# A decoder layer's weight stream: eight raw buffers of half a unit in place of four of a whole unit

## The chip, the cores and the metric

The kernel runs on one core of one Trainium2 chip. The metric is the device time of one execution in microseconds (us), the median of several runs. The core has a matrix engine (TensorE, PE in the profile; PEld is its weight load), a vector engine (VectorE, DVE), an activation engine (ScalarE, ACT), GpSimd (POOL) and SyncE (SP), which here issues nearly all loads. Transfers run on 16 DMA engines.

## The reference

A decoder layer on 256 tokens of width 1024, all in f32: a SwiGLU feed-forward, a token mixer, a second feed-forward, each behind an RMS normalisation whose shift, scale and gate come from a conditioning vector c.

```
mod = silu(c) @ w_ada + b_ada                      # 9 vectors of 1024: sh1 sc1 gt1 ... sh3 sc3 gt3
n = rmsnorm(h, g1) * (1 + sc1) + sh1
h = h + 0.5 * gt1 * ((silu(n @ w1_gate) * (n @ w1_up)) @ w1_down)        # d_ff = 2816
n = rmsnorm(h, g_mix) * (1 + sc2) + sh2
u, q, k, v = split(n @ w_in)
h = h + gt2 * (concat(pool(u), dilated_attention(q, k, v)) @ w_out)      # 8 heads of 64
n = rmsnorm(h, g2) * (1 + sc3) + sh3
h = h + 0.5 * gt3 * ((silu(n @ w2_gate) * (n @ w2_up)) @ w2_down)
out = rmsnorm(h, g_final)
```

Every matrix is f32. The kernel keeps that precision on PE by writing a matrix as a rounded part and the rest, w = hi + lo, and by three products for each: x_hi w_hi + x_lo w_hi + x_hi w_lo.

## The kernel before, in words

**Units.** The host packs all weights into 114 units of 1 MB, w[i] with 128 rows of 2048 f32 (8 KB a row), in the order in which they are used. `plan()` writes this order. Kinds of units: `ada` (two 128-column pieces of w_ada, transposed), `lead` (one eighth of the depth of four gate/up column chunks), `gu` (half the depth of one gate/up chunk), `down`, `win`, `wout`. In the first feed-forward, units 0 to 7 are ada, lead 0, ada, lead 1, ada, lead 2, ada, lead 3; two gu units follow, then ada and lead in turn again up to lead 7.

**Load and cast.** `fetch()` takes the next unit: it takes a tile `raw` of [128, 2048] from a pool of RAW = 4 buffers and SP issues one load into it (L250). For an ada unit, DVE multiplies each half with the row vector cb = silu(c) and sums along the row (L255), which gives one column of `mod` a half. For any other unit each half of 1024 columns is cast on ACT into a tile `hi` (L266), and DVE subtracts, lo = raw - hi (L267); `hi` and `lo` have PARTS = 11 buffers of half a unit each. A raw buffer goes back to the pool when both of its halves have been read, and the next load in the order waits for it on SP. `want()` fetches up to AHEAD = 5 units beyond the one that is asked for.

**The start.** Units 0 and 1 are loaded by hand, each with two loads of half a unit (L507), and a block under `in_order()` fixes the order of the first instructions of each engine as written. Unit 1's casts stand there (L544 to L555). `casts_after` keeps later casts behind that block.

**Lead steps.** For j = 0 to 3 and then 4 to 7, `lead_mod` turns two columns of mod into scale and shift (acol, L344), writes the normalised and modulated activations of depth slice j (nha on ACT, L424, then n32l on ACT and nla on DVE), and `lead_step` runs 24 matmuls (L445) on them with the lead unit: 4 chunks, 2 row tiles of 128 tokens, 3 products.

**The rest.** `ffn_chunk` (L370 to L372) and `down` (L411) run the remaining feed-forward, chunk by chunk. `finish1` and `finish2` close a sub-layer for one row tile of 128 tokens: the residual on DVE (L364, L366), squares on ACT (L294), the root on POOL (L296 to L300), scaled rows xs on ACT (L319), which PE transposes (L307). Their instructions are issued under `urgent()`, a high priority.

**Order.** Each engine executes its own queue in order. The order in a queue is fixed at compile time by a planner, which goes by the order of the code, by priorities, by added dependencies (`order_dep`, `casts_after`) and by its own model of how long loads and instructions take; it also gives out the pool buffers.

Of the kernel before, what the change touches and what calls it, by code (L numbers as in the profile page):

```python
# [10 lines left out]
F32 = mybir.dt.float32  # L11
# [4 lines left out]
P = 128  # L16
S = 256
NT = S // P
D = 1024
# [21 lines left out]
WF1 = (1, 22)  # L41
WMIX = (0, 8)
WLEAD = (0, 4)
RAW = 4
SPIN = (4, 8, 8, 5)
PARTS = 11
PAD = 336
# [8 lines left out]
def plan():  # L56
    def pairs(m):
        return [("ada", (m * KD + 2 * i, m * KD + 2 * i + 1)) for i in range(KD // 2)]

    def both(sc, sh):  # L60
        return [("ada", (sc * KD + j, sh * KD + j)) for j in range(KD)]

    def ffn(f, first):
        units = []
        for ci in range(first, NCH):
            units += [("gu", (f, ci, 0)), ("gu", (f, ci, 1))]
            if 0 < ci < NCH - HOLD + 1:
                units.append(("down", (f, ci - 1)))
        return units + [("down", (f, ci)) for ci in range(NCH - HOLD, NCH)]

    def weave(main, extra, start, stop):

        out, done = [], 0
        for i, u in enumerate(main):
            out.append(u)
            upto = min(max(i + 1 - start, 0), stop - start) * len(extra) // (stop - start)
            out += extra[done:upto]
            done = max(done, upto)
        return out

    order = []
    first, third = both(SC1, SH1), both(SC3, SH3)
    for j in range(KD):
        if j == KD // 2:
            order += [("gu", (0, ci, 0)) for ci in (4, 5)]
        order += [first[j], ("lead", (0, j))]
    f1 = [("gu", (0, ci, 1)) for ci in (2, 3)] + [("down", (0, ci)) for ci in FIRST[:-1]]
    f1 += [u if u != ("down", (0, 5)) else ("down", (0, FIRST[-1])) for u in ffn(0, 6)]
    order += weave(f1, pairs(GT1) + both(SC2, SH2) + pairs(GT2)[:EARLY], *WF1)
    mix = [("win", (ci, h)) for ci in (1, 2, 3, 0) for h in range(2)] + [("wout", i) for i in WOUT]  # L90
    order += weave(mix, pairs(GT2)[EARLY:] + third[:KD // 2], *WMIX)
    order += weave([("lead", (1, j)) for j in range(KD)], third[KD // 2:], *WLEAD)
    f2 = ffn(1, LEAD)
    f2 = f2[:2] + [("down", (1, ci)) for ci in range(LEAD - 1)] + f2[2:]
    order += weave(f2, pairs(GT3), 8, len(f2) - 8)
    return order
# [73 lines left out]
def block_kernel(ctx, tc, w, vec, x, c, gf, wpool, bandd, biasd, out):  # L170
    nc = tc.nc
    order = plan()
# [3 lines left out]
    lay = ctx.enter_context(tc.tile_pool(name="lay", bufs=1))  # L176
    rawp = ctx.enter_context(tc.tile_pool(name="rawp", bufs=RAW))
    hip = ctx.enter_context(tc.tile_pool(name="hip", bufs=PARTS))
# [38 lines left out]
    ready = {}  # L217
    bulk = []
    queues = {}
    done_mod = set()  # L220
    place = {u: i for i, u in enumerate(order)}

    def order_dep(late, early, reason):
        tc.add_manual_dep(late, early.name, mybir.DependencyInfo(
            mybir.DependencyClass.NoSync, mybir.DependencyReason.DATA), reason=reason)

    def behind(cast, unit, kind):

        units, first = queues.get(cast.ins.engine, ((1e9, 1e9), None))
        if unit >= units[kind]:  # L230
            order_dep(cast.ins, first, "casts later")

    def casts_after(firsts, units):

        for f in firsts:
            queues[f.engine] = (units, f)
        for cast in bulk:
            if any(cast[0].ins.engine == f.engine for f in firsts):
                behind(*cast)

    def note(cast, unit, kind):
        bulk.append((cast, unit, kind))
        behind(cast, unit, kind)

    def fetch():
        i = pos[0]
        pos[0] += 1
        kind, a = order[i]
        raw = rawp.tile([P, 2048], F32, name=f"raw{i}", tag="raw")
        nc.sync.dma_start(raw, w[i])  # L250
        if kind == "ada":
            with tc.high_priority(offset=ADA if i >= 2 * KD else 0):
                for s, m in enumerate(a):
                    r = raw[:, ts(s, D)]
                    note(nc.vector.tensor_tensor_reduce(  # L255
                        r, r, cb, 1.0, vecs[:, m:m + 1], ALU.mult, ALU.add, mod[:, m:m + 1]), i, 1)
                    done_mod.add(m)
            return
        his, los = [], []
        for s in range(2):  # L260
            hi = hip.tile([P, 1024], F32R, name=f"hi{i}_{s}", tag="hi")
            lo = lop.tile([P, 1024], F32R, name=f"lo{i}_{s}", tag="lo")
            n = 1024 // (2 if i in (1, 2 * KD - 1) else 1)
            for o in range(0, 1024, n):
                src = raw[:, s * 1024 + o:s * 1024 + o + n]
                note(nc.scalar.copy(hi[:, o:o + n], src), i + s / 2, 0)  # L266
                note(nc.vector.tensor_tensor(lo[:, o:o + n], src, hi[:, o:o + n].bitcast(F32), ALU.subtract), i + s / 2, 0)  # L267
            his.append(hi)
            los.append(lo)
        ready[(kind, a)] = (his, los)  # L270
# [206 lines left out]
                down(f, ci, 1, hid[ci][1], accs[1], banks)  # L477


    @contextmanager  # L480
    def in_order():

        traced = nc.cur_bb.bb.instructions
        done, last = len(traced), {}
        yield last
        for i in traced[done:]:
            if i.engine in last:
                order_dep(i, last[i.engine], "in order")
            last[i.engine] = i

    spin_ps = accp.tile([P, 2 * P], F32, name="spin", tag="acc")
    spin_in = ident.bitcast(mybir.dt.bfloat16)

# [7 lines left out]
    def x_keep(t, b, pt):  # L501
        nc.scalar.copy(xT[b][:, :, ts(t, P)], pt)

    raw = [rawp.tile([P, 2048], F32, name=f"raw{i}", tag="raw") for i in range(2)]
    for r, ww in zip(raw, (w[0], w[1])):
        for s in range(2):
            nc.sync.dma_start(r[:, ts(s, D)], ww[:, ts(s, D)])  # L507
    pos[0] = 2
    his = [hip.tile([P, 1024], F32R, name=f"hi1_{s}", tag="hi") for s in range(2)]
    los = [lop.tile([P, 1024], F32R, name=f"lo1_{s}", tag="lo") for s in range(2)]  # L510
# [4 lines left out]
    with in_order() as last:  # L515
        spin(SPIN[0])
        for b in range(2):
            pc = psp.tile([P, 512], F32, name=f"pc{b}", tag="ps")
            mm(pc, ones, crow[:, ts(b, 512)], start=True, stop=True)
            nc.scalar.activation(cb[:, ts(b, 512)], pc, AF.Silu)  # L520
        for t in range(NT):
            spin(SPIN[1 + t])
            xs.append(hip.tile([P, D], F32, name=f"xs{t}", tag="hi"))
            v = tiny.tile([P, 1], F32, name=f"vx{t}", tag="v")
            ht = h[:, ts(t, D)]
            nc.vector.tensor_tensor_reduce(xs[t], ht, ht, 1.0, D * EPS, ALU.mult, ALU.add, v)
            rs.append(tiny.tile([P, 1], F32, name=f"rx{t}", tag="r"))
            nc.gpsimd.tensor_tensor(rs[t], v, mhalf, ALU.pow)
            x_rows(t, 0)
            turned.append(turn(xs[t][:, 0:512], f"xt{t}0"))  # L530
        spin(SPIN[3])
        nc.vector.tensor_scalar(gains, vecs[:, G1:PS], float(D) ** 0.5, None, ALU.mult)
        for s, m in enumerate(order[0][1]):
            r = raw[0][:, ts(s, D)]
            nc.vector.tensor_tensor_reduce(r, r, cb, 1.0, vecs[:, m:m + 1], ALU.mult, ALU.add, mod[:, m:m + 1])
            done_mod.add(m)
        scale_cols(0, SC1, 0, 1)
        a, sh = acol[:, 0:1], mod[:, SH1 * KD:SH1 * KD + 1]
        n32 = work.tile([P, S], F32, name="n32l00", tag="t2", bufs=T2)
        for q in range(4):  # L540
            src = raw[1][:, ts(q, 512)]
            hi, lo = his[q // 2][:, ts(q % 2, 512)], los[q // 2][:, ts(q % 2, 512)]
            if q == 0:
                nc.vector.tensor_copy(hi, src)  # L544
                for t in range(NT):
                    nc.scalar.activation(n1[t][0][:, 0, :], turned[t][:, 0, :], AF.Identity, bias=sh, scale=a)
                    nc.vector.tensor_scalar(n32[:, ts(t, P)], turned[t][:, 0, :], a, sh, ALU.mult, ALU.add)
                for t in range(NT):
                    nc.vector.tensor_tensor(n1[t][1][:, 0, :], n32[:, ts(t, P)], n1[t][0][:, 0, :].bitcast(F32),
                                            ALU.subtract)  # L550
            else:
                nc.scalar.copy(hi, src)
                if q < 3:
                    x_keep(q - 1, 0, turned[q - 1])
            nc.vector.tensor_tensor(lo, src, hi.bitcast(F32), ALU.subtract)  # L555
    casts_after([last[e] for e in last if e in (nc.scalar.engine, nc.vector.engine)], (2, 2))


    nm = {}
# [305 lines left out]
```

## Time and profile before

| | before |
|---|---|
| median of 3 runs | 494.17 us (493.03 to 494.2) |
| profiled execution, its own time | 494.21 us |
| span of the profiled execution | 492.4 us |
| mean granted clock of TensorE | 0.993 |
| loads of units | 112 of 1024 KB, 4 of 512 KB |
| weight queue (q1) | 17568 packets, 121.25 MB, 65.0% of 16 engines |
| bytes read from HBM | 124.61 MB, 255 GB/s over the span with the bytes written |

The span runs from the first to the last instruction; the time of an execution lies some 1.8 us above it. Lines such as L266 are lines of the kernel before. A row of the timeline or of a group names the engine, the line, the operation, the tile that it writes and the tiles that it reads (out<-in), and in brackets the engine's idle time before it and what ended that. SPq and ACTq are the queues that issue loads.

### The profile page before, as it was taken

What the parts mean: (1) busy time and instruction counts of PE and PEld (TensorE: products, weight loads), DVE (VectorE), ACT (ScalarE), POOL (GpSimd) and SP (SyncE); (2) the same over time, 40 slices, a digit from 0 to 9 for tenths busy, and PEclk for the clock granted to TensorE, in tenths of its full rate; (3) what the DMA queues carried; (4) which work ended last, traced back from release to release, by engine and by line L of the source; (5) the groups of instructions that cost most, each with busy time, mean ns of one, the idle gap of its engine ahead of it and who ended that gap; (6) DMA issues with size and microseconds to landing.
All of it is one profiled execution on the core that took longest, in us unless ns stands there. A gap on an engine that the chain in (4) does not pass through costs nothing.

```text
span 492.4 us, 5990 instructions
## 1 busy us (share of the span) xinstructions
PE 479.4 (97%) x2176; PEld 385.1 (78%) x2176; DVE 354.8 (72%) x569; ACT 260.0 (53%) x437; POOL 15.6 (3%) x26
## 2 busy tenths in 40 slices
PE   8999999999999999899999999999999999999994
PEld 5778888888888887778767888888878888888883
DVE  5978989996897896787868776755666756655244
ACT  4776575553544354574677468945543443544121
POOL 1000000000000002120000012000000000000000
PEclk9999999999999999899999999999999999999998
DMA  8999995997987995859775848285367749540002
GB/s 306 400 359 315 369 338 203 369 425 281 396 325 286 338 385 193 309 198 405 317 244 184 298 154 318 106 321 197 126 236 253 281 189 341 180 162 9 35 2 85
DMA packets 20383, 126.05 MB, mean 256 GB/s; under 512 B 2409, under 2 KB 4225, under 8 KB 6018
## 3 DMA queue, kind: packets, MB, share of 16 engines
q1 hardware_dynamic: 17568, 121.25, 65.0%
q10 hardware_dynamic: 2786, 4.43, 2.6%
q8 instruction: 17, 0.28, 0.2%
q14 instruction: 12, 0.10, 0.1%
HBM read 124.61 MB, written 1.06 MB: 255 GB/s over the span
## 4 chain that ended last, share of the span: by engine, by line
PE 87%; DMA 5%; DVE 2%; ACT 2%; POOL 2%; issue 2%; POOLq 0%; DVEq 0%; ACTq 0%
PE accf L411 22%; PE gu L370 9%; PE le L445 9%; PE gu L371 9%; PE gu L372 9%; PE ld L445 6%; PE accm L762 5%; DMA raw<-in_w_dram 4%; PE zp L370 3%; PE zp L372 3%; PE zp L371 3%; PE ht L397 2%; DMA h<-in_x_dram 1%; ACT hi L266 1%; PE sh L370 1%
## 5 line engine op out<-in xcount | busy, mean ns | idle before, releaser
L267 DVE TENSOR_TENSOR lo<-raw,hi 128x1024 fp32r<-128x1024 f32 (+1 forms) x156 | 184.4, 1208 | 45.4 <-ACT hi L266 37.0
L266 ACT CAST hi<-raw 128x1024 fp32r<-128x1024 f32 (+1 forms) x156 | 158.3, 1041 | 78.9 <-PE accf L411 24.9
L255 DVE CUSTOM_DVE_ANT_0 raw<-raw,cb,vecs 128x1024 f32<-128x1024 f32 x70 | 88.1, 1279 | 4.8 <-DMA raw<-in_w_dram 4.8
L411 PE MATMUL accf<-hi,hh 128*128 128x512 f32 x176 | 56.3, 396 | 0.2
L411 PE MATMUL accf<-lo,hh 128*128 128x512 f32 x176 | 56.3, 394 | 0.0
L411 PE MATMUL accf<-hi,hl 128*128 128x512 f32 x176 | 55.7, 390 | 0.0
L370 PE MATMUL gu<-hi,nhc 128*128 128x512 f32 x112 | 44.4, 397 | 0.0
L372 PE MATMUL gu<-lo,nhc 128*128 128x512 f32 x112 | 43.7, 390 | 0.0
L371 PE MATMUL gu<-hi,nlc 128*128 128x512 f32 x112 | 43.7, 390 | 0.0
L388 ACT ACTIVATE sg<-gu 128x256 f32<-128x256 f32 x24 | 9.1, 381 | 65.2 <-PE gu L372 65.2
L411 PEld LDWEIGHTS accf<-hi,hl 128*128 128x128 f32 x176 | 33.0, 188 | 7.4 <-DVE hl L286 0.6
L411 PEld LDWEIGHTS accf<-lo,hh 128*128 128x128 f32 x176 | 33.3, 189 | 6.9
L411 PEld LDWEIGHTS accf<-hi,hh 128*128 128x128 f32 x176 | 32.7, 189 | 7.3 <-ACT hh L285 1.1
L391 DVE TENSOR_TENSOR pr<-sg,gu 128x256 f32<-128x256 f32 x24 | 10.0, 418 | 33.8 <-ACT sg L388 33.8
L370 PE MATMUL gu<-hi,nha 128*128 128x512 f32 x80 | 31.8, 397 | 0.0
L371 PE MATMUL gu<-hi,nla 128*128 128x512 f32 x80 | 31.2, 390 | 0.0
L372 PE MATMUL gu<-lo,nha 128*128 128x512 f32 x80 | 31.2, 390 | 0.0
L370 PE MATMUL zp<-hi,nhb 128*128 128x512 f32 x64 | 26.5, 416 | 0.0
L285 ACT CAST hh<-ht 128x256 fp32r<-128x256 f32 x44 | 14.1, 379 | 21.9 <-PE ht L397 21.9
L372 PE MATMUL zp<-lo,nhb 128*128 128x512 f32 x64 | 25.3, 395 | 0.0
L371 PE MATMUL zp<-hi,nlb 128*128 128x512 f32 x64 | 25.3, 395 | 0.0
L372 PEld LDWEIGHTS gu<-lo,nhc 128*128 128x128 f32 x112 | 21.0, 188 | 4.6
(172 smaller groups left out, 715.1 us busy)
## 6 DMA issues: line engine op xcount, KB each, us to landing
raw<-in_w_dram SPq DMA_DIRECT2D x112, 1024.0 KB, 5.1
raw<-in_w_dram SPq DMA_DIRECT2D x4, 512.0 KB, 7.7
gt<-gd ACTq DMA_DIRECT2D x3, 512.0 KB, 5.4
h<-in_x_dram SPq DMA_DIRECT2D x2, 512.0 KB
bias<-in_bias_dram ACTq DMA_DIRECT2D x4, 256.0 KB, 4.1
out_dram<-o SPq DMA_DIRECT2D x4, 160.0 KB, 2.1
bands<-in_band_dram ACTq DMA_DIRECT2D x4, 136.0 KB, 7.5
gfb<-in_gf_dram ACTq DMA_DIRECT2D x1, 512.0 KB, 4.8
```

The source lines that it names most:

```text
L255: note(nc.vector.tensor_tensor_reduce(r, r, cb, 1.0, vecs[:, m:m + 1], ALU.mult, ALU.add, mod[:, m:m + 1]), i, 1)
L266: note(nc.scalar.copy(hi[:, o:o + n], src), i + s / 2, 0)
L267: note(nc.vector.tensor_tensor(lo[:, o:o + n], src, hi[:, o:o + n].bitcast(F32), ALU.subtract), i + s / 2, 0)
L285: nc.scalar.copy(hi_ap, src)
L370: mm(ps, nh[:, k, :], whi, start=first, stop=False)
L371: mm(ps, nl[:, k, :], whi, start=False, stop=False)
L372: mm(ps, nh[:, k, :], wlo, start=False, stop=last)
L391: nc.vector.tensor_tensor(pr, sg, ps[:, 256:512], ALU.mult)
L397: nc.tensor.transpose(pt[:, i, :], pr[:, ts(i, P)], ident)
L411: mm(accs[b], a[:, k, :], cols(ww, 2 * k + b), start=st, stop=sp)
L445: mm(banks[ci][t], n[t][a][:, j, :], cols(ww, lead_set(f, j).index(ci)), start=j == 0 and p == 0, stop=last and p == 2)
L762: mm(acc2[t][b], a[:, k, :], cols(ww, 2 * kk + b), start=st, stop=sp)
```

## The change

The raw ring has eight tiles of [128, 1024] (0.5 MB each, together as many bytes as before) in place of four of [128, 2048]. A new function `load(i)` takes two tiles and issues one load of 512 KB for each: rows of 4 KB out of the 8 KB rows of w[i]. All readers of a half read its own tile, so that each half's buffer goes back to the pool by itself. The start uses the same function for units 0 and 1, which had half loads before. There are 228 weight loads in place of 116. The packed weights on the host, their order, the casts and the products are the same. The diff also moves `in_order` up, lets it remember the first instruction of each engine beside the last, and adds `casts`, `line_up` and `halves_of`, which nothing calls or reads.

```diff
-RAW = 4
+RAW = 8
...
+    casts = {}
...
+    @contextmanager
+    def in_order():
+
+        traced = nc.cur_bb.bb.instructions
+        done, last = len(traced), {}
+        yield last
+        for i in traced[done:]:
+            if i.engine in last:
+                order_dep(i, last[i.engine][1], "in order")
+            last[i.engine] = (last.get(i.engine, (i,))[0], i)
+
+    def line_up(*groups):
+
+        for (_, early), (late, _) in zip(groups, groups[1:]):
+            order_dep(late, early, "line up")
+
+    def halves_of(units, e):
+
+        return [(casts[u, s][e],) * 2 for u in units for s in range(2)]
...
+    def load(i):
+
+        raw = [rawp.tile([P, 1024], F32, name=f"raw{i}_{s}", tag="raw") for s in range(2)]
+        for s in range(2):
+            nc.sync.dma_start(raw[s], w[i][:, ts(s, 1024)])
+        return raw
+
     def fetch():
         i = pos[0]
         pos[0] += 1
         kind, a = order[i]
-        raw = rawp.tile([P, 2048], F32, name=f"raw{i}", tag="raw")
-        nc.sync.dma_start(raw, w[i])
+        raw = load(i)
         if kind == "ada":
             with tc.high_priority(offset=ADA if i >= 2 * KD else 0):
                 for s, m in enumerate(a):
-                    r = raw[:, ts(s, D)]
+                    r = raw[s]
...
-                src = raw[:, s * 1024 + o:s * 1024 + o + n]
+                src = raw[s][:, o:o + n]
                 note(nc.scalar.copy(hi[:, o:o + n], src), i + s / 2, 0)
...
+                casts[order[i], s] = bulk[-2][0].ins, bulk[-1][0].ins
...
-    raw = [rawp.tile([P, 2048], F32, name=f"raw{i}", tag="raw") for i in range(2)]
-    for r, ww in zip(raw, (w[0], w[1])):
-        for s in range(2):
-            nc.sync.dma_start(r[:, ts(s, D)], ww[:, ts(s, D)])
+    raw = [load(i) for i in range(2)]
...
-            r = raw[0][:, ts(s, D)]
+            r = raw[0][s]
...
-            src = raw[1][:, ts(q, 512)]
+            src = raw[1][q // 2][:, ts(q % 2, 512)]
...
-    casts_after([last[e] for e in last if e in (nc.scalar.engine, nc.vector.engine)], (2, 2))
+    casts_after([last[e][1] for e in last if e in (nc.scalar.engine, nc.vector.engine)], (2, 2))
```

More of the change, by code (lines that the diff above doesn't have):

```diff
@@ L477, in ffn_rest @@
                 down(f, ci, 1, hid[ci][1], accs[1], banks)
[L480 to L489, printed above, removed]
     spin_ps = accp.tile([P, 2 * P], F32, name="spin", tag="acc")
```

## The prediction

> **What bounds the kernel now.** I read the page first (span, busy time, chain), then what TensorE (PE) waited for, then all engines stage by stage, then the first 31 us row by row, then the load queue.
>
> ```profile
> span 492.4 us, 5990 instructions
> ```
>
> ```profile
> PE 479.4 (97%) x2176; PEld 385.1 (78%) x2176; DVE 354.8 (72%) x569; ACT 260.0 (53%) x437; POOL 15.6 (3%) x26
> ...
> PE 87%; DMA 5%; DVE 2%; ACT 2%; POOL 2%; issue 2%; POOLq 0%; DVEq 0%; ACTq 0%
> ```
>
> PE is busy for 97% of the span and carries 87% of the chain that ended last; transfers carry 5%, some 25 us. A change of the loads can win only where PE stands still for a weight. The waits of PE (engine, line, releaser: total, times, longest) name the places, and the stages (length; PE, PEld, DVE, ACT, POOL busy; granted clock; DMA share; GB/s) say how much it is:
>
> ```profile
> PE xtb L307 <- ACT xsb L319: 3.1, 2, 2.5
> ...
> PE ld L445 <- ACT nha L424: 1.1, 2, 0.7
> ```
>
> ```profile
> 12.00:18.00 6.00, 5.86 (x24) 4.22 (x23) 5.74 (x13) 3.48 (x7) 0.00 (x0) 1.00 1.01 427
> 18.00:24.00 6.00, 5.45 (x23) 4.19 (x24) 5.83 (x10) 5.02 (x10) 0.00 (x0) 1.00 0.95 389
> 24.00:30.00 6.00, 6.00 (x27) 4.63 (x25) 4.76 (x9) 2.78 (x5) 0.00 (x0) 1.00 0.94 328
> 30.00:36.00 6.00, 5.57 (x24) 4.18 (x24) 5.21 (x6) 5.94 (x11) 0.00 (x0) 1.00 0.94 377
> 36.00:190.00 154.00, 154.00 (x705) 127.10 (x704) 132.05 (x194) 79.44 (x121) 0.00 (x0) 1.00 0.86 330
> ```
>
> From 36 to 190 us PE has no idle time: no load, early or late, changes anything there unless PE runs dry. Between 12 and 36 us PE idles 0.14 + 0.55 + 0.00 + 0.43 = 1.12 us, and that is the field of this change: the second wait, for nha, lies there. The first one, for xsb, belongs to the normalisation between FFN and mixer, and no load releases it.
>
> **The change part by part.** *Finer release*, the part that can win. Rows picked from the timeline (start, duration, engine, line, [idle before, what ended it]), then two of the chain (start, length, what):
>
> ```profile
> 17.59 0.15 DVE L344 SCALAR_TENSOR_TENSOR acol<-mod,gains 128x1 f32<-128x1 f32 x1
> ...
> 18.00 0.88 ACT L424 ACTIVATE nha<-xT,mod,acol 128x128 fp32r<-128x128 f32 x2
> 18.13 1.23 DVE L267 TENSOR_TENSOR lo<-raw,hi 128x1024 fp32r<-128x1024 f32 x1 [0.39 <-ACT hi L266]
> ...
> 21.02 1.22 DVE L267 TENSOR_TENSOR lo<-raw,hi 128x1024 fp32r<-128x1024 f32 x1
> ...
> 22.27 1.60 SPq L250 DMA_DIRECT2D raw<-in_w_dram  x2
> ...
> 27.78 1.28 DVE L255 CUSTOM_DVE_ANT_0 raw<-raw,cb,vecs 128x1024 f32<-128x1024 f32 x1
> ...
> 29.08 1.05 ACT L266 CAST hi<-raw 128x1024 fp32r<-128x1024 f32 x1 [3.22 <-DMA raw<-in_w_dram]
> 30.03 0.87 ACT L424 ACTIVATE nha<-xT,mod,acol 128x128 fp32r<-128x128 f32 x2
> 30.57 1.35 PE L445 MATMUL ld<-hi,nha 128*128 128x512 f32 x4 [0.43 <-ACT nha L424]
> ```
>
> ```profile
> 30.57 6.02 PE ld L445 x24
> 48.44 21.76 PE ld L445 x96
> ```
>
> Unit 7 (lead 3) is the fourth load behind unit 3 and takes its buffer. It is issued at 22.27, when unit 3's second subtraction is done (21.02 + 1.22 = 22.24), and its landing ends ACT's wait at 29.08. The activation nha of lead 3 stands behind that cast on ACT, at 30.03; PE starts lead 3 at 30.57 after 0.43 us idle, and its 24 matmuls take 6.02 us. The chain's 96 undisturbed ones take 21.76, so 24 take 5.44 and 12, the work of half a unit, 2.72. Lost at lead 3: 0.43 + 0.58 = 1.01 us. With halves, unit 7's first load goes to the place that the first subtraction leaves at 18.13 + 1.23 = 19.36, 2.9 us earlier, and lands by about as much earlier. The cast then falls into the 3.22 us in which ACT idles, and nha waits only for the shift column, which DVE finishes at 27.78 + 1.28 = 29.06. With the 0.54 us that lie between 30.03 and 30.57, PE has nha at 29.60; its idle began at 30.57 - 0.43 = 30.14. So the 0.43 go, and of the 0.58 a part goes, for every lead step starts with some hesitation. I take 0.7 of the 1.01 us; the bounds are 0 and 1.01. What is late next is DVE: two products of 1.28 and two subtractions of 1.22 us are 5.0 us, with the small columns some 5.6 for each lead step of 5.44.
>
> Lead 1: unit 3's first half lands before its second, and its cast moves up. But nha at 18.00 also needs the column that DVE finishes at 17.59 + 0.15 = 17.74. At most 0.26 us go; I take 0.1. Sum: minus 0.8 us.
>
> *Twice the issues*: 112 more loads on SP.
>
> ```profile
> L250 SPq DMA_DIRECT2D raw<-in_w_dram x112: 327/328/746, 4.1 to 438.1; - x112
> ```
>
> ```profile
> SPq L250 <- DVE lo L267: 267.1, 63, 11.4
> ...
> SPq L250 <- DMA wp<-in_wpool_dram: 3.2, 1, 3.2
> ```
>
> 112 x 0.328 = 37 us of SP, hidden by the 267.1 us in which its loads wait for subtractions; without that cover they would cost 0.33 us a load. The wait for wp shows that a weight load can wait for the landing of a transfer to which it has no relation. Behind a waiting load on SP stand only further weight loads, and for those ACT's casts and DVE wait. With twice the loads such a wait may come more often. Its price to PE is zero while cast weights are in store, and up to 3.2 us without. The store, from the subtractions by stage (L267 alone; unit 1's two halves are on L555 and come on top):
>
> ```profile
> 0.00:36.00 36.00, 9.61 (x8) 1.00 0.92 355
> 36.00:100.00 64.00, 31.12 (x28) 1.00 0.87 322
> ```
>
> By 36 us 8 + 2 = 10 half units have been cast, and PE has used the 8 of four lead steps: 2 in store, 5.4 us of PE. Up to 100 us 28 more are cast while 64 us of PE use 64 / 2.72 = 23.5, so it grows to 6 or 7, some 18 us. A wait of 3.2 us is covered all along after 36 us; I cost it at 0, with +3.2 as the far bound.
>
> *Smaller pieces.* Half a unit moves rows of 4 KB in place of 8 KB. The first four loads (L507) have that size now. From 7 to 11 us they move, from 12 to 17 whole units:
>
> ```profile
> 5.00:10.00 5.00, 5.00 (x21) 3.02 (x20) 3.77 (x8) 2.05 (x4) 1.11 (x2) 1.00 1.00 356
> 7.00:11.00 4.00, 4.00 (x21) 3.27 (x20) 3.08 (x8) 1.16 (x2) 0.55 (x1) 1.00 1.04 423
> 12.00:17.00 5.00, 4.99 (x21) 3.85 (x21) 5.00 (x11) 2.53 (x6) 0.00 (x0) 1.00 1.01 426
> ```
>
> 423 / 1.04 = 407 against 426 / 1.01 = 422: a byte costs 3.7% more engine time in halves. From 12 to 30 us the transfers are busy 94 to 101%, so by unit 7 the stream may be 18 x 0.037 = 0.7 us later, out of its 2.9: nothing for PE. The first row is the far end, 356 GB/s, and makes a rival below. I take 0, by the second row, since by 7 us the queue is full of halves as it will be throughout.
>
> The Trainium skill speaks against the change here ("DMA: Bandwidth & Descriptors", Rules for kernel authors): at least 1 MiB per DMA for full bandwidth; its section on the anatomy of one DMA fits, for DMAs issued by GpSimd, 2.0 us plus bytes over 436 GB/s each. By that, loads one behind another would take an estimated 3.2 us a half and 6.4 us a unit in place of 4.4, more than the 5.44 us in which PE uses a unit, so the sum would be far above the time before. The trace does not agree while several loads are queued: 423 GB/s in halves.
>
> *Nothing else is computed*: casts, products and matmuls keep number and size; `casts`, `line_up` and `halves_of` emit no instruction and `in_order` keeps its edges: 0.
>
> *Order on ACT and DVE* is fixed at compile time, by priorities and by when the planner believes a load has landed. Halves come earlier in that belief, so a cast may get ahead of a step of a chain that PE waits for, or behind it. The trace has one such place:
>
> ```profile
> 191.76 1.28 DVE L366 TENSOR_TENSOR h<-h,resa 128x512 f32<-128x512 f32 x2
> 192.37 1.06 ACT L266 CAST hi<-raw 128x1024 fp32r<-128x1024 f32 x1 [0.30 <-PE accf L411]
> 193.33 0.63 ACT L294 ACTIVATE sqb<-h 128x512 f32<-128x512 f32 x1
> ```
>
> The first half of h is there at 191.76 + 0.64 = 192.40; the square waits behind a cast until 193.33, 0.93 us that PE stands for later. Four places are like this (two normalisations, two row tiles). No row says which way it goes: I take 0, between -0.93 and +2 x 1.06.
>
> Sum: -0.7 - 0.1 = -0.8 us. The profiled execution took 494.21 us (its span and 1.8 around it), the median of three runs is 494.17, so either will do: 494.2 - 0.8 = **493.4 us**.
>
> **The rivals.** *Hidden anyway*: DVE, at 5.6 us a lead step, is late in place of the load, and PE loses the same 1 us. For it: DVE is busy 5.83 of the 6 us from 18 on. Against it: from 24 to 30 it is busy only 4.76. No gain: 494.2 us.
>
> *Faster*: all 1.12 us of idle and lead 3's 0.58 go, and the cast at 192.37 moves behind the square: 494.2 - 1.7 - 0.9 = 491.6 us. For it: all three stand in the rows. Against it: the column at 17.74, and that the order at 192 hangs on the planner, not on the chip.
>
> *Slower, a cast ahead of the chain*: in finish1 and finish2, where ACT squares and scales while PE soon has nothing else. One more cast there (1.06 on ACT, 1.22 on DVE) eats the gain; it decides from two on: 493.4 + 2.1 = 495.5, with three 496.6. For it: one stands there now, and every landing moves. Against it: those steps are marked urgent in the code.
>
> *Slower, halves cost bandwidth*: at 356 GB/s in place of 426 the 18 us from 12 to 30 become 21.5, and unit 7's second half is 3.5 us later. PE stands for most of it: 494.2 + 3 = 497 us. It decides from a loss of some 15% on. For it: the first of the three rate rows. Against it: the second. The skill's rule of 1 MiB points the same way.
>
> **How the numbers follow.** Forecast 0.34 (its own range 492.8 to 494.0), hidden anyway 0.17, faster 0.25, cast ahead 0.17, bandwidth 0.07. About 0.3%, 1.5 us, is what the runs of this kernel (493.03 to 494.2) can tell from no change: faster lies below 492.7, slower above 495.7 or so. Faster 0.25; same 0.34 + 0.17 = 0.51; slower 0.24. The range reaches past the faster case and beyond two casts: 491.5 to 496.2, with about 0.08 left below and 0.11 above.
>
> **What would show it.** Right: unit 7's first load issued near 19.4 us, ACT's 3.22 us of waiting before the cast at 29 gone or under 1 us, PE idle under 0.2 us from 30 to 36, PE still full from 36 to 190, some 420 GB/s at 12 to 17 us. Wrong: PE waiting for hi or lo anywhere after 36 us; a longer wait for xsb or another step of the normalisation, with a cast ahead of it on ACT or DVE; a lower rate at full share in the first 30 us; lead steps that begin later because DVE puts subtractions ahead of products.

## The result, and the profile after

| | before | after |
|---|---|---|
| median of 20 runs | 494.0 us (492.67 to 497.07) | 500.07 us (493.3 to 505.6) |
| profiled execution, its own time | 494.21 us | 497.18 us |
| span, granted clock | 492.4 us, 0.993 | 495.4 us, 0.991 |

The change makes the kernel slower. The ratio is 1.0085 [1.006, 1.0109]; it leaves out the executions over 1.5% above the fastest of their kernel, so the two medians lie further apart (500.07 / 494.0 = 1.0123). The scatter has grown too: 12.3 us from the fastest to the slowest, against 4.4. The profiled execution is one of the quicker ones of its kernel, so its 3.0 us is less than the typical loss.

From the page of the changed kernel, span, busy times and the loads of units (KB each, median us from issue to landing):

```profile
span 495.4 us, 6309 instructions
...
PE 478.6 (97%) x2176; PEld 384.7 (78%) x2176; DVE 354.1 (71%) x569; ACT 260.7 (53%) x437; POOL 15.1 (3%) x26
...
raw<-in_w_dram SPq DMA_DIRECT2D x228, 512.0 KB, 6.1
```

No engine has more work: every busy time is within 0.8 us of before. What has grown is waiting. What TensorE waited for (engine, line, releaser: total, times, longest):

```profile
PE xtb L335 <- ACT xsb L347: 2.8, 2, 2.0
PE accf L439 <- DVE hl L314: 2.3, 1, 2.3
...
PE tk L335 <- ACT z L659: 1.2, 1, 1.2
...
PE ld L473 <- ACT nha L452: 0.5, 1, 0.5
```

The first row is the normalisation, as before (3.1). The last is the lead steps, halved. The two between them are new, for hl and for z, and neither is a weight. The prediction's stages, in the same columns:

```profile
12.00:18.00 6.00, 5.99 (x29) 4.69 (x28) 5.17 (x11) 4.03 (x7) 0.00 (x0) 1.00 1.03 420
...
30.00:36.00 6.00, 6.00 (x28) 4.80 (x27) 5.25 (x7) 5.84 (x10) 0.00 (x0) 1.00 1.03 400
36.00:190.00 154.00, 154.00 (x705) 127.03 (x704) 132.56 (x196) 79.88 (x121) 0.00 (x0) 1.00 0.92 332
```

The place where the change was meant to win has won: PE has no idle time from 30 to 36 us (0.43 before) and is full up to 190. The loss lies behind it. VectorE (DVE) around 366 us, where the down projection of a chunk needs hl, the rest that rounding leaves of its activations:

```profile
358.51 2.59 DVE L294 TENSOR_TENSOR lo<-raw,hi 128x1024 fp32r<-128x1024 f32 x2 [1.84 <-ACT hi L293]
362.80 1.28 DVE L282 CUSTOM_DVE_ANT_0 raw<-raw,cb,vecs 128x1024 f32<-128x1024 f32 x1 [1.71 <-DMA raw<-in_w_dram]
...
365.18 1.28 DVE L282 CUSTOM_DVE_ANT_0 raw<-raw,cb,vecs 128x1024 f32<-128x1024 f32 x1 [1.08 <-DMA raw<-in_w_dram]
...
366.39 2.35 DVE L294 TENSOR_TENSOR lo<-raw,hi 128x1024 fp32r<-128x1024 f32 x2
368.66 1.41 DVE L314 TENSOR_TENSOR hl<-ht,hh 128x256 fp32r<-128x256 f32 x4
```

DVE stands idle twice, 1.71 and 1.08 us, for the two halves of unit 96, an ada unit (in half_late96 below its products stand behind hl, and nothing after that comes late by it). Behind them in the same queue stand two subtractions, and behind those the hl that PE needs at once. Before, the order here was: subtraction, first product of 96, the four hl, subtraction, second product. PE at the same place (start, duration):

```profile
365.59 1.20 PE L439 MATMUL accf<-hi,hh 128*128 128x512 f32 x4
369.13 0.73 PE L439 MATMUL accf<-hi,hl 128*128 128x512 f32 x2 [2.34 <-DVE hl L314]
...
371.43 1.05 PE L439 MATMUL accf<-lo,hh 128*128 128x512 f32 x2
...
374.94 0.61 PE L439 MATMUL accf<-lo,hh 128*128 128x512 f32 x2
```

PE stops for 2.34 us, and then it is slow: the same pair of matmuls takes 1.05 us in place of 0.61. The windows of 2 us say why (the column behind POOL is the granted clock):

```profile
368.00:370.00 2.00, 0.87 (x4) 0.74 (x5) 2.00 (x5) 0.00 (x0) 0.00 (x0) 1.00 0.95 279
370.00:372.00 2.00, 2.00 (x8) 1.59 (x7) 0.07 (x1) 0.00 (x0) 0.00 (x0) 0.66 0.82 279
372.00:374.00 2.00, 2.00 (x7) 1.51 (x6) 0.00 (x0) 0.63 (x1) 0.00 (x0) 0.50 0.46 184
374.00:376.00 2.00, 2.00 (x10) 1.67 (x9) 1.55 (x2) 1.28 (x2) 0.00 (x0) 0.99 0.02 8
```

The clock falls to 0.66 and 0.50 of full speed from 370 to 374 us, which costs 2 x 0.34 + 2 x 0.50 = 1.7 us. Stop and slow clock together are 4.0 us. The other new wait, on ScalarE (ACT):

```profile
230.90 1.05 ACT L293 CAST hi<-raw 128x1024 fp32r<-128x1024 f32 x1 [2.91 <-DMA raw<-in_w_dram]
231.85 0.59 ACT L659 ACTIVATE z<-zp 128x512 f32<-128x512 f32 x1
```

The same place before:

```profile
231.30 0.60 ACT L645 ACTIVATE z<-zp 128x512 f32<-128x512 f32 x1 [2.88 <-PE zp L372]
232.11 2.00 ACT L266 CAST hi<-raw 128x1024 fp32r<-128x1024 f32 x2 [0.22 <-DMA raw<-in_w_dram]
```

A cast of a weight half has come ahead of z; ACT idles until that half lands, and z, for which PE waits, starts 0.55 us later than before, in a kernel that was 2 us ahead of before until then (table below).

To see where time goes between two kernels I set the start of their n-th matmul side by side (both have 2176). Each number is how much later than before's profile (positive) or earlier (negative) a kernel is when before stands at that time. The experiments' kernels are in the same table:

| us of before | 33.5 | 203.6 | 221.4 | 238.7 | 264.0 | 287.3 | 366.2 | 375.6 | end |
|---|---|---|---|---|---|---|---|---|---|
| after | -0.24 | -2.00 | -2.06 | -0.64 | -1.69 | -1.40 | -1.22 | +2.75 | +2.73 |
| half_again | -1.00 | -1.24 | -1.43 | +0.10 | -0.96 | +4.24 | +4.45 | +8.23 | +8.23 |
| half_oldorder | -0.97 | -0.85 | -0.88 | +0.93 | +0.91 | +0.89 | +1.84 | +1.85 | +1.87 |
| whole_twoloads | -1.08 | -1.00 | -1.00 | -0.47 | -0.48 | -0.50 | -0.55 | -0.54 | -0.52 |
| half_late96 | -1.16 | -1.40 | -1.62 | +2.06 | +0.98 | +1.43 | +1.62 | +1.77 | +1.78 |
| half_mended | -0.97 | -2.73 | -2.77 | -2.13 | -3.24 | -3.01 | -2.77 | -2.61 | -0.96 |
| whole_96ahead | +0.22 | -1.31 | -1.20 | -1.20 | -1.20 | -1.20 | -1.18 | +4.61 | +4.61 |
| whole_twoloads_free | -0.97 | -2.91 | -2.71 | -0.31 | -0.82 | -1.15 | +2.58 | +3.46 | +3.46 |
| half_mended4 | -1.05 | -0.28 | -0.49 | -0.39 | -1.47 | -1.16 | -0.93 | -0.75 | -0.75 |

After gains ahead of 204 us, loses 1.4 at z (221 to 239) and 4.0 at hl (366 to 376).

Most of the gain ahead of 204 us is not the change's. In the normalisation between feed-forward and mixer PE stops for xsb, and in before's profile the clock then runs at half:

```profile
200.00:202.00 2.00, 2.00 (x8) 1.62 (x8) 0.63 (x2) 2.00 (x6) 0.00 (x0) 0.50 1.06 434
```

In after's profile it is 1.00 there; in half_again's, the same kernel with the same stop of 2.01 us, it is 0.50 from 198 to 200 us. The slow stretch costs before 2 x (0.32 + 0.50 + 0.03) = 1.7 us from 198 to 204 us. whole_96ahead has before's order up to 366 us and the same stop of 2.46 us, but no slow clock behind it, and goes from +0.22 to -1.31 here. So these 1.7 us come and go between executions, and each number from 203.6 us on has them in it or not.

### The profile page after: what moved, and what is told of

Its sections match the earlier page's. It is cut to its first block, busy times and chain, and to the rows that moved or that the text cites. A ratio compares the mean times of both kernels' runs of the same rounds, so it can differ in the third digit from the quotient of the medians.

```text
span 495.4 us, 6309 instructions
## 1 busy us (share of the span) xinstructions
PE 478.6 (97%) x2176; PEld 384.7 (78%) x2176; DVE 354.1 (71%) x569; ACT 260.7 (53%) x437; POOL 15.1 (3%) x26
## 3 DMA queue, kind: packets, MB, share of 16 engines
HBM read 124.61 MB, written 1.06 MB: 254 GB/s over the span
## 5 line engine op out<-in xcount | busy, mean ns | idle before, releaser
L314 DVE TENSOR_TENSOR hl<-ht,hh 128x256 fp32r<-128x256 f32 x44 | 16.4, 415 | 11.4 <-ACT hh L313 11.4
```

Of the source, the lines that this page charges most:

```text
L314: nc.vector.tensor_tensor(lo_ap, src, hi_ap.bitcast(F32), ALU.subtract)
```

## The experiments

Two theories. *Queue order (Q)*: the planner believes that a half load lands sooner, orders ACT and DVE by that belief, and puts readers of loads that are still on their way ahead of the z, nly and hl that PE waits for. *The loads themselves (L)*: 512 KB pieces and eight buffers make the stream slower or its landings later, whatever the order. The order can be pinned: a kernel carries a list of places for each engine and chains its instructions by it, so that another kernel's order is kept (the lists, ORDER, are left out here).

```diff
+    placed = {}
+    for i in nc.cur_bb.bb.instructions:
+        if not type(i).__name__.startswith("BassTile"):
+            placed.setdefault(str(i.engine).split(".")[-1], []).append(i)
+    for e, runs in ORDER.items():
+        queue = [placed[e][s + k] for s, n in runs for k in range(n)]
+        for early, late in zip(queue, queue[1:]):
+            order_dep(late, early, "order")
```

| kernel | loads and ring | order | median us | before, run beside it | ratio [95%] |
|---|---|---|---|---|---|
| half_again | halves, 8 | planner | 502.68 (one run) | 493.48 | - |
| half_oldorder | halves, 8 | before's | 494.39 | 493.48 | 1.0009 [0.9993, 1.0024] |
| whole_twoloads | halves, 4 whole | before's | 493.63 | 493.48 | 0.9999 [0.9987, 1.0012] |
| half_late96 | halves, 8 | after's, one move | 496.24 | 493.48 | 1.0044 [1.0019, 1.0069] |
| half_mended | halves, 8 | after's, three moves | 494.14 | 493.98 | 1.0008 [0.9986, 1.0031] |
| half_mended4 | halves, 8 | after's, four moves | 493.73 | 493.09 | 1.0007 [0.9986, 1.0028] |
| whole_96ahead | whole, 4 | before's, one move | 499.42 | 493.98 | 1.0116 [1.0092, 1.0141] |
| whole_twoloads_free | halves, 4 whole | planner | 499.75 | 493.98 | 1.0111 [1.0085, 1.0136] |

**half_again**: the changed kernel once more, no edit, for a second profile.

> The changed kernel unchanged, for a second profile, since its runs lie between 493 and 506 us and the one profiled (497.2) is among the lower. Theory Q (order: casts and products of late loads stand ahead of steps that PE needs, on ACT and DVE): the loss sits in a few PE waits, each with a cast or product that waited for a load ahead of it on ACT or DVE; the places are the same as in the first profile (z near 230 us, hl near 366 us), the lengths differ. Theory L (half loads are slow in themselves): PE waits for hi or lo, or the loss is spread over the span.

It took 502.68 us. What PE waited for:

```profile
PE pt L695 <- DVE nly L729: 3.0, 1, 3.0
...
PE accf L439 <- DVE hl L314: 2.2, 1, 2.2
...
PE tk L335 <- ACT z L659: 1.4, 1, 1.4
```

DVE before the longest of them, and the clock behind it:

```profile
279.71 1.28 DVE L282 CUSTOM_DVE_ANT_0 raw<-raw,cb,vecs 128x1024 f32<-128x1024 f32 x1 [3.34 <-DMA raw<-in_w_dram]
...
280.92 0.86 DVE L729 SCALAR_TENSOR_TENSOR nly<-pw,vecs,nhy 128x128 fp32r<-128x128 f32 x3
```

```profile
282.00:284.00 2.00, 1.99 (x9) 1.26 (x8) 0.66 (x2) 0.93 (x3) 0.00 (x0) 0.60 0.78 258
284.00:286.00 2.00, 2.00 (x7) 1.42 (x6) 0.58 (x2) 0.53 (x2) 0.00 (x0) 0.55 0.23 53
```

The stops for hl and z are there again, at the same places. A third, at nly, is not in the first profile: again a product of an ada unit (unit 80) stands ahead, and its second half landed 8.4 us after its issue, against a median of 6.2. It costs 5.2 us (264 to 287 us in the table). So the places are fixed by the order, and how long PE stands at each hangs on when a load happens to land. That fits the scatter of 12.3 us; two profiles don't prove it for every run.

**half_oldorder**: all of the change, but each engine's order as in before (ORDER from before; the chain above).

> The half loads and the ring of eight, but every instruction of PE, ACT, DVE and POOL in the order that the kernel before has. Theory Q: 492.5 to 494 us, spread as small as before's; the 1 us won in the lead steps stays, the waits for z near 230 and hl near 366 us are gone. Theory L: 497 us or more, with the old order's steps waiting for late halves.

494.39 us, ratio 1.0009 [0.9993, 1.0024], 0.4 us above what Q expected. The group of DVE's ada products, whose last column is the idle time ahead of them, tells the same. Before, after, and half_oldorder, one row each:

```profile
L255 DVE CUSTOM_DVE_ANT_0 raw<-raw,cb,vecs 128x1024 f32<-128x1024 f32 x70 | 88.1, 1279 | 4.8 <-DMA raw<-in_w_dram 4.8
```

```profile
L282 DVE CUSTOM_DVE_ANT_0 raw<-raw,cb,vecs 128x1024 f32<-128x1024 f32 x70 | 88.5, 1279 | 11.0 <-DMA raw<-in_w_dram 11.0
```

```profile
L350 DVE CUSTOM_DVE_ANT_0 raw<-raw,cb,vecs 128x1024 f32<-128x1024 f32 x70 | 88.1, 1278 | 1.7 <-DMA raw<-in_w_dram 1.7
```

With halves in the new order DVE stands 11.0 us (15.6 in half_again) for landings in front of its products; with the same halves in the old order 1.7. The loss follows the order. Two waits are new even so in this profile, which is that of the slowest of the twelve runs (496.47 us): 1.6 us for z near 228 and 0.9 us for nhc near 298 us. The trace doesn't lay them to a weight half. Ahead of z, ACT stands for `bands`, a small load that ACT issues itself:

```profile
225.03 1.45 ACTq L782 DMA_DIRECT2D wp<-in_wpool_dram  x1
226.52 1.04 ACT L361 CAST hi<-raw 128x1024 fp32r<-128x1024 f32 x1 [4.92 <-DMA bands<-in_band_dram]
```

Ahead of nhc it stands 5.97 us for `gfb`, another small load (3.92 before). Whether the halves make these land later is open; whole_twoloads, next, has halves and the same order and neither wait.

**whole_twoloads**: four whole buffers as before, before's order (by the chain above), only each unit's load cut in two.

```diff
-        nc.sync.dma_start(raw, w[i])
+        for s in range(2):
+            nc.sync.dma_start(raw[:, ts(s, D)], w[i][:, ts(s, D)])
```

> The kernel before with its ring of four whole buffers and its order on all engines, but each unit with two loads of 512 KB, one right behind the other. Theory Q: as before, 493.5 to 495 us. Theory L: 497 us or more; the two halves of a unit land later than the whole did.

0.9999 [0.9987, 1.0012]: 228 loads of 512 KB cost no time by themselves. Its stage from 36 us on:

```profile
36.00:190.00 154.00, 154.00 (x703) 127.06 (x702) 132.77 (x195) 78.92 (x121) 0.00 (x0) 1.00 0.91 331
```

Halves do cost the DMA engines something: 330 GB/s at a busy share of 0.86 before, 331 at 0.91 here, 332 at 0.92 in the changed kernel, 6% more engine time for a byte. There is room for it, and PE is full. The Trainium skill's rule of at least 1 MiB per DMA for bandwidth ("DMA: Bandwidth & Descriptors", Rules for kernel authors) holds in that sense only; no run here shows it in the time. And the table has -1.08 us at 33.5 us: the gain in the lead steps is all there without the finer release. ACT in this kernel:

```profile
26.63 1.06 ACT L335 CAST hi<-raw 128x1024 fp32r<-128x1024 f32 x1 [0.95 <-DMA raw<-in_w_dram]
...
28.91 0.88 ACT L493 ACTIVATE nha<-xT,mod,acol 128x128 fp32r<-128x128 f32 x2 [1.23 <-DVE mod L324]
```

The first half of unit 7 is cast at 26.63 (29.08 before), because it signals its own landing; nha then waits for DVE's column. By 239 us half of this gain is lost again in this profile: at 233.94 us a cast that has stood 1.74 us for a landing is ahead of kT on ACT, and PE waits 0.28 us for kT. The 0.5 us that are left are less than the median can show, with an interval of 0.6 us to either side.

**half_late96**: after's order, with only unit 96's two products moved behind the four hl on DVE.

> The changed kernel in its own order, but for one move on DVE: the two products of unit 96 stand behind the four hl of the second feed-forward's first chunks instead of ahead of them. Theory Q: PE's wait of 2.3 us near 366 us and the slow clock behind it go, 3 to 4.5 us off the profiled execution's span (about 491.5), and the median falls from 500 to 496 or so. Theory L: hl still late, or the loss turns up at the next step; the median stays at 499 or more.

496.24 us, 1.0044 [1.0019, 1.0069]. The hl wait is gone from PE's waits, and from 366 to 376 us the kernel loses 0.15 where after lost 3.97. In this profile z costs more, 3.7 us from 221 to 239: 1.9 of waiting, and a clock of 0.59 and 0.55 from 234 to 238 us. By the ratios (1.0085 to 1.0044, each against its own runs of before) the move of one unit's products gives back about half of the loss, though the two intervals overlap; the rest is at the other places.

**half_mended** and **half_mended4**: three moves (unit 96 behind hl, unit 80 and its column behind nly, the first cast of unit 69 behind z), then a fourth (unit 105's products behind hl of another chunk).

> The changed kernel in its own order, but for three moves: the two products of unit 96 behind the four hl near 366 us (as before), the products of unit 80 with their acol behind the pooling mixer's nly near 280 us (both on DVE), and the cast hi of unit 69's first half behind z21 near 232 us (on ACT). These are the three places where PE waited over 1 us more than before in the two profiles of the changed kernel (497.2 and 502.7 us). Theory Q: PE waits at none of the three, median 492 to 493.7 with a small spread, since the lead steps' 1 us and the normalisation's 0.5 to 1 us stay won. Theory L: other steps wait for late halves instead, 495 us or more.

494.14 us, 1.0008 [0.9986, 1.0031], so three moved spots take the loss away within the interval. Q had expected less, 492 to 493.7, and a small spread; it is 6.0 us, against 3.4 of before's runs beside it. PE waits at none of the three places. What was still late, PE's wait and DVE ahead of it in half_mended's profile:

```profile
PE accf L507 <- DVE hl L382: 1.3, 1, 1.3
```

```profile
402.34 1.28 DVE L350 CUSTOM_DVE_ANT_0 raw<-raw,cb,vecs 128x1024 f32<-128x1024 f32 x1 [4.94 <-DMA raw<-in_w_dram]
```

The same pattern a fourth time, with unit 105: 1.65 us from 376 to 411 in the table. In the fourth kernel that is moved too:

> As the one with three moves (494.1 us), with a fourth on DVE: both products of unit 105 behind the two hl of chunk 5, near 405 us, where the profile of the three moves shows DVE waiting 4.94 us for that unit's load and PE then 1.3 us for hl. Theory Q: PE does not wait there, 1.5 to 2 us less than with three moves, median 492 to 493, which would be faster than before. If late halves keep finding other steps: 494 us again, with a wait at another place.

493.73 us, 1.0007 [0.9986, 1.0028]. Its profile has no wait for hl, z or nly any more and ends 0.75 us earlier than before's, but the median isn't the 492 to 493 that Q expected: no version here beats before. Earlier parts vary by more than what is to be won. At 203.6 us, behind a normalisation with the same order, half_mended is 2.7 us ahead and half_mended4 0.3. PE's stop for xsb took 2.01 us in the one and 2.99 in the other, and only half_mended4 has the slow clock behind it (1.00 in half_mended):

```profile
200.00:202.00 2.00, 2.00 (x6) 1.53 (x5) 1.50 (x3) 2.00 (x4) 0.00 (x0) 0.50 0.70 279
```

**whole_96ahead**: the kernel before with whole loads, and on DVE only the order at unit 96 as the change has it.

> The kernel before (whole loads, ring of four) in its own order, but for one place on DVE near 366 us, which has the changed kernel's order: both products of unit 96, then two subtractions, then the four hl. If the order alone costs the time: PE waits for hl as in the changed kernel, 2.3 us and the slow clock behind it, 497 us or so. If it needs the order and the late half load together: the whole unit 96, issued at 356.2 us, has landed by 361.5, DVE does not wait, and hl is late by 1 us at most: 493.5 to 495 us.

499.42 us, 1.0116 [1.0092, 1.0141]: no half load in it beyond the four that before has, and it is as slow as the change. I had taken an earlier load for unit 96's, whose own goes out at 359.8 us, and expected too little. PE's wait, DVE, and the clock:

```profile
PE accf L479 <- DVE hl L354: 3.2, 1, 3.2
```

```profile
364.88 1.28 DVE L323 CUSTOM_DVE_ANT_0 raw<-raw,cb,vecs 128x1024 f32<-128x1024 f32 x1 [3.75 <-DMA raw<-in_w_dram]
...
369.57 1.41 DVE L354 TENSOR_TENSOR hl<-ht,hh 128x256 fp32r<-128x256 f32 x4
```

```profile
370.00:372.00 2.00, 1.96 (x5) 1.58 (x6) 0.98 (x3) 0.00 (x0) 0.00 (x0) 0.50 1.01 397
372.00:374.00 2.00, 2.00 (x6) 1.56 (x5) 0.00 (x0) 0.00 (x0) 0.00 (x0) 0.50 0.98 393
374.00:376.00 2.00, 2.00 (x7) 1.57 (x6) 0.00 (x0) 0.44 (x1) 0.00 (x0) 0.63 0.15 61
```

The stop of 3.2 us and 2 x (0.50 + 0.50 + 0.37) = 2.7 us of slow clock are 5.9; the table has 5.8 (366 to 376 us). With whole loads the bad order costs more than with halves, for the first product can start at 364.88, where the first half of the unit let it start at 362.80.

**whole_twoloads_free**: whole_twoloads without the pinned order, so that the planner chooses.

> The kernel before with its ring of four whole buffers and two loads of 512 KB a unit, the planner free to order as it likes. Its order on DVE then differs from before's in some 68 places, on ACT in 32, against 83 and 37 in the changed kernel. If it is smaller loads that make the planner choose a bad order: 496 us or more, with a spread as large as the changed kernel's. If it takes the ring of halves: 493 to 495 us.

499.75 us, 1.0111 [1.0085, 1.0136], with the ring of whole buffers. PE's waits:

```profile
PE tk L308 <- ACT z L646: 2.2, 1, 2.2
PE le L446 <- ACT nhc L286: 1.8, 1, 1.8
...
PE accf L412 <- DVE hl L287: 0.8, 1, 0.8
```

Pinned and free, the same loads and the same buffers, differ by 1.1% (0.9999 and 1.0111). So cutting the loads is enough to make the planner choose a costly order; the ring of halves isn't needed for it. (The spread, 2.8 us in six runs, is not the large one that was expected.) Two of the waits are of the kind seen above: ahead of z a cast had stood 4.05 us for a landing, ahead of hl a product 2.60 us. The third, for nhc, costs most, 3.7 us from 287 to 366 in the table, and no landing is in it: three casts stand ahead on ACT (293.66 to 296.59 us; two in before) and run without a wait, the root on GpSimd took 1.55 us in place of 0.55, and behind the stop the clock is 0.50 from 300 to 302 us.

Q stands as to the order; that each costly place is a late landing holds for the changed kernel's z, nly and hl, not for nhc here. L is refuted as to the time, to within the intervals of half_oldorder and whole_twoloads. PE's own order differs in the changed kernel too, but half_mended keeps that order and is as fast as before, and whole_96ahead has before's and is slow: it isn't what costs.

## Why the prediction was wrong

The forecast was 493.4 us, its range ended at 496.2; the median is 500.07.

*Order on ACT and DVE* is the step that failed: "I take 0, between -0.93 and +2 x 1.06." It named the mechanism and had the wrong places and the wrong size. It looked at the normalisations, where a cast (1.06 us) is the price. They did little harm: in the first PE's longest wait for xsb is 2.0 us in the changed kernel, 2.5 before, and in the second PE waits 0.2 us for nhc. The harm lies where a *load* stands between: an ada product or a cast that is put too early doesn't cost its own 1.3 or 1.06 us, it costs the wait for its landing (1.71 and 1.08 at unit 96, 3.34 at unit 80, 2.91 at z), and then the slow clock. One such place came to 4.0 and 5.2 us, more than the whole upper bound of 2.1. None of the prediction's signs of being wrong names such a place. DVE's timeline of before had the pair to ask about, one of these products directly ahead of hl:

```profile
366.31 1.28 DVE L255 CUSTOM_DVE_ANT_0 raw<-raw,cb,vecs 128x1024 f32<-128x1024 f32 x1
...
367.51 1.41 DVE L286 TENSOR_TENSOR hl<-ht,hh 128x256 fp32r<-128x256 f32 x4
```

Had I listed which readers of `raw` stand next to hl, nly and z, and how soon after its landing each starts, the bound would have been a landing and not a cast.

The rival "a cast ahead of the chain" was right in kind and too low, 495.5 to 496.6. As it was told, in a normalisation and without a landing, it came about in whole_twoloads_free alone, at nhc, and cost more than its casts there too.

*Finer release*: unit 7's first load goes out at 19.73, predicted 19.36; PE's idle time at lead 3 is gone; the gain was put at 0.8 and is 0.97 to 1.16 in all seven other kernels with half loads (whole_96ahead, with whole ones, has none). In the changed kernel's own profile some 0.8 us had been lost in the start already, behind a GpSimd step: ACT scales the rows from 7.89 us on, in half_again from 6.93. ACT's wait went from a landing to DVE's column, as was said of what is late next. But the size came right for a reason that isn't needed: in whole_twoloads unit 7 is issued at 22.08 us, as late as before, and the stage wins as much, because the half's own landing is enough.

*Twice the issues*: 0 was right. No hi or lo stands in PE's waits, with 112 more issues.

*Smaller pieces*: 0 was right, and the size too: from 12 to 18 us 420 / 1.03 = 408 GB/s at full share against 427 / 1.01 = 423, so 3.7% dearer, as was read off; later 6%.

*Nothing else is computed*: right, by the busy times.

## What to carry to other kernels

Where a planner orders in-order queues by its own idea of when loads land, a change of the load size can change the order on several engines (here TensorE, VectorE and ScalarE); compare the two orders before costing the loads, and look for readers of loads just ahead of what the bounding engine needs next. To tell an edit from the reordering that comes with it, pin the old order and measure the edit alone, then the new order alone. A reader of a load that has slack belongs behind the urgent step, for a misplaced one can cost the wait for a landing, not its own duration. Before a difference of 1 or 2 us between two profiles is put down to an edit, compare the granted clock behind each stop.

## What the runs showed of the hardware

Halving a load didn't halve its time to landing: the median from issue was 6.1 us for 512 KB with eight in the ring, 6.1 for 512 KB in a ring of four units, against 5.1 for 1024 KB before (5.5 in whole_96ahead).

A stop of TensorE of 2.34 us was followed by 2 x (0.34 + 0.50) / 0.5 = 3.4 us at half the clock, one of 3.2 us by 2.74 / 0.5 = 5.5 us of it. With the slow clock these two stops cost 1.7 and 1.8 times their length (4.0 / 2.34, 5.8 / 3.2). That isn't a fixed price. A stop of 2.46 us was followed by the half clock in before (0.50 from 200 to 202 us) and not in whole_96ahead (1.00), one of 2.01 us in half_again (0.50 from 198 to 200 us) and not in the same kernel's other profile, after (1.00). What decides it is open. The Trainium skill ("TensorE: Matmul & The Clock Gate", What's actually happening) has half rate after an idle window of about 3.4 us; the rate agrees with the 0.50, but here shorter stops, 2.01 and 2.34 us, were enough.
